# Up projections of two MLPs: five groups of 1024 columns each computed as seven half-size products, spread among plain tiles

## The chip, the cores and the metric

The kernel runs on one core of one Trainium2 chip. The metric is the time of one execution on the device in microseconds (us), median of several runs. TensorE (PE in the profile, with PEld for its weight loads) multiplies, VectorE (DVE) and ScalarE (ACT) work element by element, GpSimd (POOL) does little here, and SyncE (SP) issues the loads of the weights. SBUF is the memory that the engines read; PSUM holds the results of matmuls.

## The reference

The reference is a trunk of two layers on 256 tokens of width 2048, all in float32. Layer 0 mixes tokens by stick-breaking attention (mixer A), layer 1 by an attention over selected keys (mixer B). After each mixer comes an MLP with 8192 hidden features. The part that matters:

```python
for i in range(DEPTH):                      # 2 layers
    h = rms_norm(x, norm_mix[i])
    x = x + mixer(h, ...)                   # A in layer 0, B in layer 1
    h = rms_norm(x, norm_mlp[i])
    x = x + jnp.square(jax.nn.relu(h @ w_up[i])) @ w_down[i]
    # x (256, 2048), w_up (2048, 8192), w_down (8192, 2048)
```

## The kernel before

All weights pass through the core once, in pieces of 512 KB called items. An item is a tile of 128 partitions by 1024 float32 numbers. `load` (L674, its issue is L679) fetches it with SP's queue into one of five raw buffers (wraw). `split` (L681) takes it apart into a high part wh, which ScalarE writes by a copy that rounds (L82), and a low part wl, which VectorE writes as the difference (L689). Both lie in one buffer w, of which there are three. The matmuls then take x_hi·wh + x_hi·wl + x_lo·wh, which gives nearly float32 accuracy from three products in the rounded format. The activations are kept as high and low parts too.

There are two forms of item:

- `feats_out` (L201) gives features on partitions: the weights are stationary, 128 columns at a time, and x moves. An item covers four k-tiles and 256 columns: 8 pairs of a matmul of 512 columns (wh by x_hi and x_lo side by side, L211) and one of 256 (wl by x_hi, L212). It is used for the up projections and the features of the mixers.
- `tokens_out` (L178) gives tokens on partitions: x or h is stationary and the weights move. An item covers two k-tiles and 512 columns: 2 halves of the tokens x 2 k-tiles x 3 matmuls of 512 columns (L192 to L194).

In `mlp` (L250) the 8192 hidden features are taken in four parts of 2048. For each part come 32 up items (eight groups of 256 columns, four items each) and then 32 down items. When a group of the up projection is complete, `up_done` (L262) joins its two accumulators (ScalarE copy and VectorE add), squares the relu (VectorE), and writes high and low parts into hT (ScalarE, VectorE). hT is then stationary for the down projection. `down_done` (L272) adds the result to the residual stream xs, scaled by rs2, the square of the normalisation factor. The normalisation itself is left out of the MLP's operand and applied there, since relu squared is homogeneous. `prep` (L124) transposes xs with TensorE (L131) and writes xT, the split operand of the next projections.

The items of both layers stand in one list. The loop at the end of `trunk` walks through it: for item i it emits the split of item i + 2 (LEAD), the load of item i + 7 (LEAD + RAW), the matmuls of item i, and what has been put behind it (`post`). Only the first 16 items keep this order as written, and what is wrapped in `keep_in_program_order`; else a planner chooses the order of the instructions on each engine, by its own costs. PSUM has three accumulators of two banks (accp) and two of one bank (auxp).

The kernel's few lines that set the pace of an item:

```python
pair = wpool.tile([P, 2 * WT + BANK], F32R, name="w")        # three of these
copy(wh, raw)                                                # ScalarE
pin(dve.tensor_sub(wl, raw, wh.bitcast(F32)))                # VectorE
```

## Time and profile before

| what | value |
|---|---|
| runs, us | 2124.61, 2124.94, 2125.48; median 2124.94 |
| span of the profiled execution, first to last instruction | 2123.1 us |
| the profiled execution's own time | not listed apart; the runs lie 1.5 to 2.4 us above the span |
| TensorE busy | 2112.1 us, 99%, 10772 matmuls |
| VectorE busy | 1248.9 us, 59%, 1397 instructions |
| ScalarE busy | 1007.7 us, 47%, 1274 instructions |
| read from memory | 391.8 MB, 187 GB/s over the span |
| granted TensorE clock | 1.000 |

A row of a group names the line, the engine, the operation, what is written from what, the shapes and the count; then the busy time, the mean of one instruction in ns, and the idle time of the engine just before them with what ended it. A row of the timeline begins with start and duration in us. A row of windows gives a stretch, its length, and busy time with count of instructions for TensorE, its weight loads, VectorE, ScalarE and GpSimd, then the granted clock, the share of the DMA engines and GB/s. A row of waits says which engine and line waited for which, the total in us, how often, and the longest. A row of DMA issues ends with the KB of one and the median us from issue to landing. L82 is the line of the helper `copy`, which all ScalarE copies share.

### The profile page before, as it was taken

Reading aid. Unit: us, or ns where it says so; the run is one execution under the profiler, and the core shown is the slowest. Engines: PE = TensorE matmul, PEld = TensorE weight load, DVE = VectorE, ACT = ScalarE, POOL = GpSimd, SP = SyncE. Lnnn points to the kernel's source line nnn. Section 1 sums busy time; section 2 is a strip of 40 time slices with the busy share of each in tenths; the row PEclk is TensorE's granted clock in tenths of the full one; section 3 lists DMA queues with packets and bytes.
Section 4 is the critical chain, followed back from the end, with each engine's and each line's share of the span. In section 5 each row is a group of like instructions: output and inputs, shape, how many; then the busy total and the mean of one; then the engine's idle time right before and its main releaser. Section 6 shows DMA issues by size and latency. Waiting matters only on the chain.

```text
span 2123.1 us, 27404 instructions
## 1 busy us (share of the span) xinstructions
PE 2112.1 (99%) x10772; PEld 1800.8 (85%) x10772; DVE 1248.9 (59%) x1397; ACT 1007.7 (47%) x1274; POOL 28.3 (1%) x71
## 2 busy tenths in 40 slices
PE   8999999999999999999999999999999999999999
PEld 7888888888888888888888788888888888888887
DVE  5456665665565456456555877666555555555654
ACT  5455554544444444344454556555434434434443
POOL 0101100000000000000000000000000000000000
PEclk9999999999999999999999999999999999999999
DMA  7667655666666666666666565456666666666664
GB/s 238 189 194 192 180 165 177 184 190 194 193 189 192 194 190 190 194 190 189 193 213 183 159 193 164 149 179 188 193 194 189 191 193 191 190 195 192 188 205 151
DMA packets 298742, 398.93 MB, mean 188 GB/s; under 512 B 14578, under 2 KB 195444, under 8 KB 298612
## 3 DMA queue, kind: packets, MB, share of 16 engines
q1 hardware_dynamic: 290852, 389.74, 60.8%
q10 hardware_dynamic: 7760, 7.43, 1.3%
q8 instruction: 84, 1.38, 0.3%
q14 instruction: 46, 0.38, 0.1%
HBM read 391.82 MB, written 5.23 MB: 187 GB/s over the span
## 4 chain that ended last, share of the span: by engine, by line
PE 99%; DMA 0%; DVE 0%; ACT 0%; DVEq 0%; issue 0%
PE acc L211 29%; PE acc L192 17%; PE acc L193 17%; PE acc L194 17%; PE acc L212 15%; PE aux L131 1%; PE aux L589 0%; PE aux L193 0%; PE aux L194 0%; PE aux L192 0%; PE aux L370 0%; PE acc L326 0%; PE acc L503 0%; PE aux L606 0%; PE aux L567 0%; PE acc L468 0%
## 5 line engine op out<-in xcount | busy, mean ns | idle before, releaser
L689 DVE TENSOR_TENSOR w<-wraw,w 128x1024 fp32r<-128x1024 f32 x738 | 903.5, 1224 | 706.5 <-ACT w L82 697.0
L82 ACT ACTIVATE w<-wraw 128x1024 fp32r<-128x1024 f32 x738 | 782.4, 1060 | 835.5 <-PE acc L194 513.3
L211 PE MATMUL acc<-xT,w 128*128 128x512 f32 x2688 | 934.8, 390 | 0.0
L212 PE MATMUL acc<-xT,w 128*128 128x256 f32 x2688 | 759.0, 282 | 0.0
L211 PEld LDWEIGHTS acc<-xT,w 128*128 128x128 f32 x2688 | 504.6, 188 | 104.6
L212 PEld LDWEIGHTS acc<-xT,w 128*128 128x128 f32 x2688 | 508.0, 189 | 1.0
L192 PE MATMUL acc<-w,hT 128*128 128x512 f32 x992 | 386.3, 389 | 0.0
L194 PE MATMUL acc<-w,hT 128*128 128x512 f32 x992 | 386.2, 389 | 0.0
L193 PE MATMUL acc<-w,hT 128*128 128x512 f32 x992 | 385.9, 389 | 0.0
L194 PEld LDWEIGHTS acc<-w,hT 128*128 128x128 f32 x992 | 186.2, 188 | 38.7
L192 PEld LDWEIGHTS acc<-w,hT 128*128 128x128 f32 x992 | 186.2, 188 | 38.6
L193 PEld LDWEIGHTS acc<-w,hT 128*128 128x128 f32 x992 | 186.2, 188 | 38.2
L192 PE MATMUL acc<-w,xT 128*128 128x512 f32 x320 | 127.5, 399 | 2.5 <-ACT w L82 2.5
L193 PE MATMUL acc<-w,xT 128*128 128x512 f32 x320 | 126.5, 395 | 0.5 <-DVE w L689 0.5
L194 PE MATMUL acc<-w,xT 128*128 128x512 f32 x320 | 126.2, 394 | 0.0
L82 ACT ACTIVATE jc<-acc 128x512 f32<-128x512 f32 x84 | 50.4, 600 | 128.1 <-PE acc L212 128.0
L193 PE MATMUL acc<-w,oT 128*128 128x512 f32 x256 | 101.3, 396 | 0.0
L192 PE MATMUL acc<-w,oT 128*128 128x512 f32 x256 | 101.1, 396 | 0.0
L194 PE MATMUL acc<-w,oT 128*128 128x512 f32 x256 | 100.7, 394 | 0.0
L224 DVE TENSOR_TENSOR ju<-acc,jc 128x512 f32<-128x512 f32 x80 | 55.3, 691 | 77.0 <-ACT jc L82 77.0
L192 PEld LDWEIGHTS acc<-w,xT 128*128 128x128 f32 x320 | 60.6, 189 | 17.3 <-ACT w L82 2.9
L193 PEld LDWEIGHTS acc<-w,xT 128*128 128x128 f32 x320 | 60.5, 189 | 13.0 <-DVE w L689 1.0
(145 smaller groups left out, 1033.0 us busy)
## 6 DMA issues: line engine op xcount, KB each, us to landing
wraw<-in_w_up_dram SPq DMA_DIRECT2D x256, 512.0 KB, 3.8
wraw<-in_w_down_dram SPq DMA_DIRECT2D x256, 512.0 KB, 4.9
wraw<-in_w_in_a_dram SPq DMA_DIRECT2D x96, 512.0 KB, 4.3
wraw<-in_w_in_b_dram SPq DMA_DIRECT2D x64, 512.0 KB, 3.8
wraw<-in_w_out_a_dram SPq DMA_DIRECT2D x32, 512.0 KB, 3.7
wraw<-in_w_out_b_dram SPq DMA_DIRECT2D x32, 512.0 KB, 4.0
bv_d<-bv ACTq DMA_DIRECT2D x4, 766.0 KB, 9.0
bias<-bv_d ACTq DMA_DIRECT2D x4, 512.0 KB, 5.3
```

Of the source, the lines that this page charges most:

```text
L82: pin(act.activation(o, i, AF.Copy, scale=scale))
L131: pin(pe.transpose(ps[:, j, t * P:(t + 1) * P], xs[:, t, kt * P:(kt + 1) * P], ident))
L192: pin(pe.matmul(acc[t], L[:, k, 0, ts], wh[:, j, :], start=(k == 0), stop=False))
L193: pin(pe.matmul(acc[t], L[:, k, 0, ts], wl[:, j, :], start=False, stop=False))
L194: pin(pe.matmul(acc[t], L[:, k, 1, ts], wh[:, j, :], start=False, stop=(k == KT - 1)))
L211: pe.matmul(acc[:, m, :], wh[:, j, ms], xT[:, k, :, :], start=(k == 0), stop=False)
L212: pe.matmul(acc[:, m, 0:S], wl[:, j, ms], xT[:, k, 0, :], start=False, stop=(k == KT - 1))
L224: dve.tensor_add(u, acc[:, :, :S], c)
L689: pin(dve.tensor_sub(wl, raw, wh.bitcast(F32)))
```

## The change

Five groups of 1024 columns of each up projection are computed by Strassen's scheme in the variant with seven products and shared sums (Winograd's form). The operand x is cut in tokens (two halves of 128) and in k (two halves of 1024), the weights in k and in columns (two halves of 512). Instead of eight products of halves there are seven, of sums of quarters. The other 3072 columns of a layer remain plain: 1024 at the start, and 512 with each of the first four groups (hR).

- `forms` makes the four sums of x's quarters once per layer (xS, high and low parts), behind items 5 to 12 of the plain start.
- `seven` gives for a group 16 items (`first`) and 12 items (`second`), each with 6 matmuls of 512 columns with tokens on partitions. Per step of two k-tiles, four blocks of weights are loaded, b11 into wraw, b12, b22 and b21 into two new raw buffers (sraw). `sums` and `last_sum` replace blocks in place by sums on VectorE before they are split. A block can serve several items, so a raw buffer is given back only after its last use (`uses`, `loads`).
- Products that belong to several quarters of the result are kept apart in PSUM and combined on VectorE and ScalarE (`between`, `between2`, `after`, `after2`), squared (`square_up`), transposed by TensorE to features on partitions and split into hS (`turn`).
- The 28 half items of a group are spread among the down items of the group before and the plain up items (`spread`, SPANS). The down projection takes 1024 or 1536 rows at a time (hS, hR) in place of 2048.
- `prep` scales xs by the old normalisation factor before the MLP's transposes (two more ScalarE copies a chunk), and `stats` takes that out again.
- To make room in SBUF, some constants move to a pool that ends with the first section, RS moves into the sections, and smaller buffers are shared.

```diff
+HK = KT // 2
+LASTF = 5
+SPANS = {24: (11, 6), 32: (15, 8)}
+RAWS = {"wraw": RAW, "sraw": 2}
...
     def prep(c, col, squares=True, halves=(0, 1)):
 
+        block = [xs[:, t, c * 512:(c + 1) * 512] for t in range(2)]
+        if col >= 64:
+            for t in range(2):
+                even = tmp.tile([P, 2, S], F32, name="jc").rearrange("p a b -> p (a b)")
+                copy(even, block[t], scale=rs[:, t:t + 1])
+                block[t] = even
...
         def stats():
+            back = tmp.tile([P, 2], F32, name="back")
+            dve.reciprocal(back, rs)
             row_scale()
             sec["rs2"] = tmp.tile([P, 2], F32, name="rs2")
-            dve.tensor_mul(sec["rs2"], rs, rs)
+            dve.tensor_mul(sec["rs2"], rs, back)
+            dve.tensor_mul(sec["rs2"], sec["rs2"], sec["rs2"])
+        def whole(b, half):
+            t = sec["a", half] = temp().rearrange("p (k t) -> p k t", k=4)
+            ks = slice(HK * half + 4 * b, HK * half + 4 * b + 4)
+            dve.tensor_add(t, xT[:, ks, 0, :].bitcast(F32), xT[:, ks, 1, :].bitcast(F32))
+        def mixed(b, n):
...
+            if n == 0:
+                dve.tensor_sub(d(0), a21, a22)
+            elif n == 1:
+                dve.tensor_sub(d(1), d(0), a11)
+            elif n == 2:
+                dve.tensor_sub(d(2), a11, a21)
+            else:
+                dve.tensor_add(d(3), a12, d(1))
+        def parted(b, m):
+            d, x = sec["d", m], sec["xS"][:, 2 * m:2 * m + 2, 4 * b:4 * b + 4]
+            for n in range(2):
+                copy(x[:, n, :, 0, :], d[:, n])
+            for n in range(2):
+                dve.tensor_sub(x[:, n, :, 1, :], d[:, n], x[:, n, :, 0, :].bitcast(F32))
...
+        def seven(f, c0):
...
+            def item(raws, bank, x, s, source, opens=True):
+                def mm(wh, wl):
+                    acc = bank()
+                    on = dict(skip_group_check=not opens)
+                    for j in range(KB):
+                        k = KB * s + j
+                        pe.matmul(acc, x(k, 0), wh[:, j, :], start=opens and k == 0, stop=False, **on)
+                        pe.matmul(acc, x(k, 0), wl[:, j, :], start=False, stop=False, **on)
+                        pe.matmul(acc, x(k, 1), wh[:, j, :], start=False, stop=k == HK - 1, **on)
+                return Item(raws, KB, 512, mm, True, source)
...
+            for s in range(HK // KB):
+                b11, b12 = block(0, 0, s, "wraw"), block(0, 1, s, "sraw")
+                b21, b22 = block(1, 0, s, "sraw"), block(1, 1, s, "sraw")
+                def sums(s=s, b11=b11, b12=b12, b22=b22):
+                    t = g["t", s] = temp().rearrange("p (a b) -> p a b", a=KB)
+                    dve.tensor_add(b11.ap, b11.ap, b12.ap)
+                    dve.tensor_add(b12.ap, b12.ap, b22.ap)
+                    dve.tensor_add(t, b11.ap, b22.ap)
+                    return b12.ap
+                def last_sum(s=s, b21=b21):
+                    dve.tensor_add(b21.ap, g["t", s], b21.ap)
+                    return b21.ap
+                first += [item([b11], pair(0), quarter(0, 0), s, lambda b=b11: b.ap),
+                          item([b22, b12], single("v"), summed(3), s, lambda b=b22: b.ap),
+                          item([], pair(1), summed(2), s, sums),
+                          item([], single("z"), summed(0), s, lambda b=b11: b.ap)]
+                first[-2].uses = [b11, b12, b22]
+                first[-1].uses = [b11]
+                second += [item([b21], single("y"), quarter(1, 0), s, lambda b=b21: b.ap),
+                           item([], pair(0), summed(1), s, lambda s=s: g["t", s], False),
+                           item([], pair(1), quarter(1, 1), s, last_sum, False)]
+                second[-1].uses = [b21]
...
+            def between():
+                copy(se(0), pair(0)())
+                g["s5"] = flat("jc")
+                copy(g["s5"], g["z"])
+            def between2():
+                dve.tensor_sub(se(1), g["s5"], pair(1)())
+                dve.tensor_add(se(2), g["s5"], g["v"])
+            def after():
+                g["s2"] = flat("jc")
+                copy(g["s2"], pair(0)())
+                dve.tensor_sub(se(2), se(2), pair(0)())
+                dve.tensor_sub(se(1), se(1), pair(0)())
+            def after2():
+                dve.tensor_add(g["s2"], pair(1)(), g["s2"])
+                dve.tensor_add(se(0), g["y"], se(0))
+            def square_up(c):
+                dve.scalar_tensor_tensor(c, c, 0.0, c, op0=OP.max, op1=OP.mult)
+            def turn(c0, c1, kt):
+                h = h_tile(f, "hS")
+                ps = auxp.tile([P, 2, S], F32, name="aux")
+                for j in range(2):
+                    for t, c in enumerate((c0, c1)):
+                        cs = slice((kt + j) % 4 * P, ((kt + j) % 4 + 1) * P)
+                        pe.transpose(ps[:, j, t * P:(t + 1) * P], c[:, cs], ident)
+                hi = h[:, kt:kt + 2, 0, :]
+                copy(hi, ps)
+                dve.tensor_sub(h[:, kt:kt + 2, 1, :], ps, hi.bitcast(F32))
...
+        base = [0] + [1024 + 1536 * n for n in range(LASTF)]
+        items = up(0, "hS", 0, 4, 2)
         items[2 * QA + 1].post.append(stats)
+        todo = forms()
+        put(items, 5, [lambda n=n: (todo[2 * n](), todo[2 * n + 1]()) for n in range(8)])
+        for f in range(LASTF):
+            ds = down(f, base[f], ("hS",) if f == 0 else ("hS", "hR"))
+            if f + 1 < LASTF:
+                ds += up(f + 1, "hR", base[f + 1] + 1024, 2)
+            first, second, mid, ends = seven(f + 1, base[f + 1])
+            n1, n2 = SPANS[len(ds)]
+            items += spread(first, ds[:n1])
+            at = len(items) - 1
+            items += ds[n1:n1 + 2] + spread(second, ds[n1 + 2:n1 + 2 + n2])
+            put(items, at, mid)
+            at = len(items) - 1
+            items += ds[n1 + 2 + n2:]
...
+            for n, which in enumerate(((0, 1), (2,), (3, 4), (5,), (6, 7))):
+                items[at + n].post += [ends[e] for e in which]
+        items += down(LASTF, base[LASTF], ("hS",))
         return items, begin
...
+    def loads(done, most=None):
+        n, full = 0, set()
+        for raw in list(queue):
+            if n == most or raw.first > done + RAW + 3:
+                return
+            before = ahead[raw.tag]
+            if len(before) >= RAWS[raw.tag] and before[-RAWS[raw.tag]].last > done:
+                full.add(raw.tag)
+            if raw.tag not in full:
+                queue.remove(raw)
+                before.append(raw)
+                load(raw)
+                n += 1
```

More of the change, by code (lines that the diff above doesn't have):

```diff
@@ L99, in trunk @@
     dve.tensor_copy(tri, trif)
-    ones = consts.tile([P, P], F32R, name="ones")
+    ones = early.tile([P, P], F32R, name="ones")
     dve.tensor_copy(ones, onesf)
@@ L176, in rows, with tokens_out @@
         return w[r0:r0 + nr, c0:c0 + ncol].rearrange("(a p) c -> p a c", p=P)
-    def tokens_out(items, key, w, r0, c0, lhs, q, done, apart=False):
+    def tokens_out(items, key, w, r0, c0, lhs, q, done, n=KT, apart=False):
         def mm(wh, wl):
@@ new lines, in parted, with forms @@
+        def parted(b, m):
[4 more added lines that the diff above has]
+                dve.tensor_sub(x[:, n, :, 1, :], d[:, n], x[:, n, :, 0, :].bitcast(F32))
+        def forms():
+            out = []
+            for b in range(2):
+                out += [lambda b=b: whole(b, 0), lambda b=b: whole(b, 1)]
+                out += [lambda b=b, n=n: mixed(b, n) for n in range(4)]
+                out += [lambda b=b: parted(b, 0), lambda b=b: parted(b, 1)]
+            return out
@@ new lines, in up_done, with h_tile @@
+        def up_done(h, s, acc):
+            u = joined(acc)
+            dve.scalar_tensor_tensor(u, u, 0.0, u, op0=OP.max, op1=OP.mult)
+            hi = h()[:, 2 * s:2 * s + 2, 0, :]
+            copy(hi, u)
+            dve.tensor_sub(h()[:, 2 * s:2 * s + 2, 1, :], u, hi.bitcast(F32))
+        def h_tile(f, kind):
+            if (f, kind) not in sec:
+                n = {"hS": HK, "hR": 4}[kind]
+                sec[f, kind] = sec["pool"].tile([P, n, 2, S], F32R, name=kind, bufs=2 if kind == "hS" else 1)
+            return sec[f, kind]
@@ new lines, in down @@
+        def down(f, r0, kinds):
+            its, parts = [], [(k, i) for k in kinds for i in range({"hS": HK, "hR": 4}[k])]
+            n = len(parts)
+            for g in range(4):
+                for q in range(n // KB):
+                    tokens_out(its, ("dn", g), w_down[l], r0, 512 * g,
+                               lambda k, part, ts: sec[f, parts[k][0]][:, parts[k][1], part, ts], q,
+                               lambda acc, g=g: down_done(f, g, acc), n,
+                               apart=next_col is None and (f, g) == (LASTF, 3))
+            return its
@@ L272, in down_done @@
         def down_done(f, g, acc):
[L273 to L274 removed]
+            if f < LASTF or next_col is not None:
+                add_residual(g, next_col if f == LASTF else None, acc, sec["rs2"])
                 return
@@ L671, in trunk, with load, split @@
         n += len(its)
-    raws, parts = {}, {}
-    def load(i):
+    parts = {}
+    queue = []
+    for i, it in enumerate(items):
+        queue += it.raws
+        for raw in it.raws:
+            raw.first = i
+        for raw in getattr(it, "uses", it.raws):
+            raw.last = i
+    ahead = {tag: [] for tag in RAWS}
+    def load(raw):
+        home = wpool if raw.tag == "wraw" else now[0]
+        raw.ap = home.tile([P, WT], F32, name=raw.tag, bufs=RAWS[raw.tag])[:, :raw.a * raw.b].rearrange(
+            "p (a b) -> p a b", a=raw.a)
+        pin(nc.sync.dma_start(raw.ap, raw.src))
+    def loads(done, most=None):
[10 more added lines that the diff above has]
+                load(raw)
+                n += 1
+    def split(i):
         if i < len(items):
             it = items[i]
-            raws[i] = wpool.tile([P, WT], F32, name="wraw", bufs=RAW)[:, :it.a * it.b].rearrange(
-                "p (a b) -> p a b", a=it.a)
-            pin(nc.sync.dma_start(raws[i], it.src))
-    def split(i):
-        if i < len(items):
-            it, raw = items[i], raws.pop(i)
             pair = wpool.tile([P, 2 * WT + BANK], F32R, name="w")
@@ L697, in trunk @@
     for i in range(RAW):
-        load(i)
+        loads(-1, 1)
         if i == 0:
@@ L706, in trunk @@
         split(i)
-        load(RAW + i)
+        loads(i, 1)
     items[0].post.append(lambda: prep(0, 0, False, (1,)))
@@ L718, in trunk @@
         split(i + LEAD)
-        load(i + LEAD + RAW)
+        loads(i + LEAD)
         it.mm(*parts.pop(i))
```

155 lines of the change are left out of this document (104 added, 51 removed).

## Prediction

> **What bounds the kernel now.** I read the page's head and its chain of waits first, then what TensorE waited for, then its starts in both kinds of tile, and last VectorE.
>
> ```profile
> span 2123.1 us, 27404 instructions
> PE 2112.1 (99%) x10772; PEld 1800.8 (85%) x10772; DVE 1248.9 (59%) x1397; ACT 1007.7 (47%) x1274; POOL 28.3 (1%) x71
> PE 99%; DMA 0%; DVE 0%; ACT 0%; DVEq 0%; issue 0%
> PE acc L192 <- ACT w L82: 2.5, 1, 2.5
> PE acc L193 <- DVE w L689: 0.5, 1, 0.5
> ACT w L82 <- PE acc L212: 271.2, 174, 2.6
> ```
>
> The chain lies on TensorE, which after the first microseconds waited 3 us in all for a split weight tile (L192, L193). Splitting goes the other way: ScalarE waits for TensorE to give back one of three w buffers. So TensorE's own starts set the time. A busy TensorE is modelled with overlapping matmuls, so I take distances between starts, not durations. First and last rows of two stretches, down projection and up projection:
>
> ```profile
> 499.81 0.39 PE L194 MATMUL acc<-w,hT 128*128 128x512 f32 x1
> ...
> 511.82 0.39 PE L193 MATMUL acc<-w,hT 128*128 128x512 f32 x1
> ...
> 599.82 0.39 PE L211 MATMUL acc<-xT,w 128*128 128x512 f32 x1
> 600.05 0.28 PE L212 MATMUL acc<-xT,w 128*128 128x256 f32 x1
> ...
> 605.71 0.39 PE L211 MATMUL acc<-xT,w 128*128 128x512 f32 x1
> ```
>
> The first stretch holds 54 matmuls: 12.01/53 = 0.2266 us for 512 columns. The second holds 18 of L211: 5.89/17 = 0.3465 us for a pair of 512 and 256. A down item (12 matmuls) is 2.72 us, an up item (8 pairs) 2.77.
>
> The sum is made against the profiled execution: span 2123.1, and 1.5 to 2.4 us outside it, since the runs shown lie at 2124.61 to 2125.48 (the time of that very execution is not listed apart). I use the median, 2124.9, as span plus 1.8.
>
> **What the change takes from TensorE.** A group of 1024 columns is now 16 up items, 128 pairs: 44.35 us. After it is 28 half items of 6 matmuls of 512 columns (7 products, 8 k-tiles each, 3 matmuls a k-tile): 168 x 0.2266 = 38.07. Saved 6.28 a group, 62.8 over ten groups (five in each of two layers).
>
> **What it adds there.** The halves come out with tokens on partitions, so each group turns 16 tiles back in four blocks of four. The nearest rows are the turns of xs between matmuls:
>
> ```profile
> 1384.93 0.48 PE L192 MATMUL acc<-w,oT 128*128 128x512 f32 x1
> 1385.25 0.81 PE L131 MATMUL aux<-ident,xs 128*128 128x128 f32 x6
> 1385.82 0.48 PE L193 MATMUL acc<-w,oT 128*128 128x512 f32 x1
> 1386.14 0.39 PE L194 MATMUL acc<-w,oT 128*128 128x512 f32 x1
> ```
>
> From 1384.93 to 1386.14 is 1.21 us, of which two matmuls are 0.45, so six turns cost 0.76: 0.095 each and 0.19 for going in and out. Four cost 0.57, a group 2.28, all 22.8. Bounds: 15.2 without the going in and out; about 44 at the recorded 277 ns each, which pipelining excludes here. I take 22.8, the row that is the same operation. TensorE is left with 62.8 - 22.8 = **40.0 us less: 2085**, if it never waits.
>
> **What it adds on VectorE and ScalarE.** Rows for the pieces; the first four show VectorE's starts:
>
> ```profile
> 608.28 0.69 DVE L224 TENSOR_TENSOR ju<-acc,jc 128x512 f32<-128x512 f32 x1 [1.09 <-ACT jc L82]
> 609.01 0.69 DVE L267 SCALAR_TENSOR_TENSOR sq<-ju 128x512 f32<-128x512 f32 x1
> 609.62 1.22 DVE L689 TENSOR_TENSOR w<-wraw,w 128x1024 fp32r<-128x1024 f32 x1
> 610.75 0.68 DVE L270 TENSOR_TENSOR hT<-sq,hT 128x512 fp32r<-128x512 f32 x1
> ...
> L689 DVE TENSOR_TENSOR w<-wraw,w 128x1024 fp32r<-128x1024 f32 x738 | 903.5, 1224 | 706.5 <-ACT w L82 697.0
> L82 ACT ACTIVATE w<-wraw 128x1024 fp32r<-128x1024 f32 x738 | 782.4, 1060 | 835.5 <-PE acc L194 513.3
> L82 ACT ACTIVATE jc<-acc 128x512 f32<-128x512 f32 x84 | 50.4, 600 | 128.1 <-PE acc L212 128.0
> L559 DVE TENSOR_TENSOR nr<-nr,nry 128x1024 f32<-128x1024 f32 x5 | 6.1, 1221 | 0.1
> L233 DVE SCALAR_TENSOR_TENSOR xs<-acc,rs,xs 128x512 f32<-128x512 f32 x56 | 39.5, 747 | 11.3 <-PE acc L194 11.3
> ```
>
> An operation on 128x1024 takes 1.22 us as recorded but the next starts after 1.13; on 128x512 it is 0.69 recorded, 0.61 to the next start, 0.73 where the next needs the result. So every piece has two prices. A group's 28 splits and 16 sums of weight blocks (three in sums, one in last_sum, four times) are 44 x 1.13 = 49.7, and 14 operations at its end (between2, after, after2, the squares, the turns' low parts) x 0.65 = 9.1: 58.8 us (63.5 recorded), where 16 splits and four up_done were 16 x 1.13 + 12 x 0.65 = 25.9. The forms add 4 x 1.13 + 16 x 0.65 = 14.9 us a layer. VectorE so rises from 1249 by ten times 33 to 36 and 30, to some 1610 to 1640 of 2090 us: 78%, not the bound on average.
>
> Locally it is nearer. I call what lies between two groups' ends a period: 28 half items and the plain ones spread among them. Up_done costs 2.0 on VectorE, a finished down group 1.4:
>
> - first period (16 down, 8 up): TensorE 38.1 + 43.5 + 22.2 + 2.3 = 106.1; VectorE 58.8 + 24 x 1.13 + 4.0 + 5.6 = 95.5, 90% (103.0 recorded, 97%).
> - three periods of 24 down, 8 up: TensorE 127.9; VectorE 104.6, 82% (112.8, 88%).
> - last (24 down): TensorE 105.7; VectorE 91.5, 87% (98.9, 94%).
>
> ScalarE in the densest has 52 x 1.06, 7 x 0.60 and two up_done of 1.23: 62 of 106 us. No bound. Loads stay 16 of 512 KB a group; 40 in 106 us are 198 GB/s, beside 191 at a DMA share of 0.63 in this row, so bandwidth isn't the bound either:
>
> ```profile
> 1600.00:1800.00 200.00, 200.00 (x1038) 172.19 (x1037) 113.33 (x111) 88.78 (x93) 0.00 (x0) 1.00 0.63 191
> 1190.00:1200.00 10.00, 10.00 (x54) 7.77 (x51) 8.73 (x25) 5.89 (x8) 0.00 (x0) 1.00 0.44 117
> 1200.00:1210.00 10.00, 10.00 (x46) 8.27 (x45) 10.00 (x34) 4.14 (x5) 0.00 (x0) 1.00 0.67 201
> 1210.00:1220.00 10.00, 10.00 (x46) 8.29 (x45) 8.52 (x19) 4.65 (x6) 0.00 (x0) 1.00 0.71 204
> ```
>
> The last three rows are mixer B's top-k: VectorE 27.25 of 30 us busy (91%), once 10 of 10, and TensorE starts 46 matmuls in 10 us, no fewer than 0.2266 allows. Splits ran between the top-k operations:
>
> ```profile
> 1202.55 1.22 DVE L689 TENSOR_TENSOR w<-wraw,w 128x1024 fp32r<-128x1024 f32 x1
> ...
> 1204.08 0.62 DVE L525 MAX8 m<-sc 128x8 f32<-128x128 f32 x2
> ...
> 1205.25 1.22 DVE L689 TENSOR_TENSOR w<-wraw,w 128x1024 fp32r<-128x1024 f32 x1
> ```
>
> So 2.70 us apart, the pace of an item, while other work waited. The planner, which orders all this by itself, puts urgent splits ahead; I expect the same of sums and forms (forms bring 15 us of VectorE work into eight items, but nothing reads them before the second half item).
>
> **What a wait costs.** A split needs a w buffer back, then ScalarE, then VectorE:
>
> ```profile
> 602.15 1.06 ACT L82 ACTIVATE w<-wraw 128x1024 fp32r<-128x1024 f32 x1 [1.71 <-PE acc L212]
> 603.24 1.23 DVE L689 TENSOR_TENSOR w<-wraw,w 128x1024 fp32r<-128x1024 f32 x1 [1.54 <-ACT w L82]
> ```
>
> 602.15 to 604.47 is 2.32 us. With three buffers it may begin when the item three before ends and must be done when the one before ends: two items' time. Plain tiles give 5.44 - 2.32 = 3.1 us of slack; a half and a plain 4.08 - 2.32 = 1.8; two halves side by side 2.72 - 2.32 = 0.4. In-order VectorE has nothing behind a late operation but the next split, which TensorE waits for. By the order of spread, side-by-side halves occur 5 + 6 times in a dense period and 1 + 4 in the others: 37 a layer, 74 in all. Other work than splits holds VectorE for (95.5 - 52 x 1.13)/106 = 35% of a dense period; a running 1.13 us sum hurts when more than 0.4 of it is left (65%), by 0.37 on average: 74 x 0.35 x 0.65 x 0.37 = 6 us. Two more places, where a group's end is followed by the tiles that read it (turned hS, first item of down; after the last period only one plain item covers the turns), I put at 1 us a layer each: 4. Bounds: nothing, and 74 x 0.73 = 54 if each of those meets a whole sum. I take 10, near the top-k rows, where a fuller VectorE cost nothing.
>
> The even copies in prep are two more ScalarE copies of 128x512 per chunk of x at the mixers' ends. The last chunk is first read by the seventh item of the up projection, so six items, 16 us of matmuls, hide them; uncovered they would cost 1.4 us for the last chunk of each layer, 2.8 in all. The pool moves, RS's new place and the reciprocal in stats are off the path. The tail after the last matmul is unchanged.
>
> **Forecast**: 2124.9 - 40.0 + 10 = **2095**, its own range 2083 to 2108. Chance 0.62.
>
> **Rivals.**
> - *VectorE at its recorded durations.* If operations are held by each other so that the overlap of 0.09 us is lost, and 91% is the most that leaves TensorE fed, then the first period takes 103.0/0.91 = 113.2 (+7.1), the last 108.7 (+3.0), the plain start with forms (16 x 1.224 + 8.3 + 16.0 + 1)/0.91 = 49.3 against 44.3 (+5.0), the middle none: 15.1 a layer, 30 in all: **2115**. For: sums follow one another in place. Against: the top-k rows at 10 of 10. Chance 0.22, a third of it above 2120.7. The Trainium skill ("VectorE: DVE Perf Modes", The DRAIN you can't avoid) says a next operation does not start until the pipe has emptied, though one that isn't held starts earlier; by that rule alone this rival is the result. The trace agrees with the exception: 609.62 to 610.75 is less than 1.22.
> - *The two sraw buffers, a slower kernel.* b12 and b22 of the next step can be loaded only when the sums and the third item's split have read the old ones, and SP's queue holds later loads behind that wait. The loop: issue and landing, a second block behind it, split, two sums, copy, split. Landings:
>
> ```profile
> wraw<-in_w_up_dram SPq DMA_DIRECT2D x256, 512.0 KB, 3.8
> wraw<-in_w_down_dram SPq DMA_DIRECT2D x256, 512.0 KB, 4.9
> ```
>
> A block at full share is 0.524/(191/0.63) = 1.7 us, so 4.9 + 1.7 + 2.32 + 2.26 + 2.2 = 13.4 at most; with sums running before the second block's split less. TensorE's work per step is 4 x 1.36 + 2.75 x 2.72 = 12.9 in dense periods (16 steps), 15.6 in others (24). It decides from 15.4 on (16 x 2.5 = 40). At 16, with a load queued behind two others, it costs 16 x 3.1 + 24 x 0.4 = 59: **2144**. For: 13.4 exceeds 12.9 already. Against: such a chain must miss the prefetch in every step, and bandwidth is a third free. Chance 0.14.
> - *No waits at all, turns cheaper*: below 2083, chance 0.02.
>
> **How the numbers follow.** This kernel's runs tell 0.2% (4.2 us) from no change. Faster: 0.62 + 0.02 + two thirds of 0.22 = 0.79; within: 0.07; slower: 0.14. The range 2083 to 2127 leaves out 0.02 below and the slow rival above.
>
> **What would show it.** Pairs of L211 and L212 fall from 2688 to 1408 each, and 1680 matmuls of 512 columns stand in their place at 0.227 us: else the saving is wrong. Turns in four blocks of 0.57. VectorE at 76 to 79% of the span. TensorE's waits for w (from the split's sums) at 5 to 20 us in all, short, and mostly at side-by-side halves. I am wrong if those waits exceed 40 us, if SP's loads end them, if VectorE is full for whole periods, or if the turns cost twice as much.

## The result, and the profile after

The changed kernel takes 2104.05 us (median of 4 runs, 2102.72 to 2105.25). The kernel before, run beside it, takes 2125.06 (2124.61 to 2125.48). The ratio is 0.9901 with a 95% interval of 0.9887 to 0.9915: faster by 21 us, 1%. Forecast were 2095, a range of 2083 to 2108, and a gain of 30.

The head of the page with its chain, and three waits that the change could have touched, two of TensorE's and one of ScalarE's for a load (who waited for which, us in total, times, longest):

```profile
span 2101.4 us, 26497 instructions
PE 2080.6 (99%) x10052; PEld 1736.0 (83%) x10052; DVE 1614.7 (77%) x1773; ACT 1141.6 (54%) x1416; POOL 28.1 (1%) x71
PE 94%; DVE 4%; issue 1%; ACT 1%; DMA 0%; DVEq 0%; ACTq 0%
```

```profile
PE acc L217 <- DVE w L941: 9.3, 15, 1.9
PE acc L216 <- ACT w L100: 3.1, 3, 2.5
ACT w L100 <- DMA wraw<-in_w_up_dram: 1.7, 1, 1.7
```

L217 is the old L193, L941 the old L689 (VectorE's half of a split), L100 the old L82 (ScalarE's copies). The chain is still TensorE's, but 4% of it now runs over VectorE, where it was 0%. The wait for the low part of a weight tile has gone from 0.5 us to 9.3. For a load of the up projection ScalarE waited once, 1.7 us.

The groups of the pairs that remain, of the splits, and of the sums:

```profile
L941 DVE TENSOR_TENSOR w<-wraw,w 128x1024 fp32r<-128x1024 f32 x658 | 801.4, 1223 | 349.7 <-ACT w L100 342.9
L238 PE MATMUL acc<-xT,w 128*128 128x512 f32 x1408 | 494.7, 392 | 0.0
L239 PE MATMUL acc<-xT,w 128*128 128x256 f32 x1408 | 398.5, 284 | 0.0
...
L395 DVE TENSOR_TENSOR t<-wraw,sraw 128x1024 f32<-128x1024 f32 x40 | 48.7, 1218 | 0.0
L394 DVE TENSOR_TENSOR sraw<-sraw 128x1024 f32<-128x1024 f32 x40 | 48.8, 1220 | 0.3
```

L238 and L239 are the old L211 and L212: 1408 each, as predicted. Three windows (length; busy time and count of TensorE, weight loads, VectorE, ScalarE, GpSimd; clock, DMA share, GB/s): the stretch with `forms`, one inside the first period (from one group's first half item to the next group's), and one later on:

```profile
385.00:430.00 45.00, 45.00 (x247) 39.08 (x246) 39.00 (x56) 26.89 (x41) 0.00 (x0) 1.00 0.64 197
480.00:540.00 60.00, 57.99 (x268) 47.43 (x267) 51.68 (x52) 31.68 (x33) 0.00 (x0) 1.00 0.58 185
580.00:680.00 100.00, 100.00 (x478) 83.81 (x478) 83.17 (x83) 54.20 (x56) 0.00 (x0) 1.00 0.60 194
```

VectorE is 87, 86 and 83% busy. TensorE is idle in the middle one alone, for 2.01 us. So the idle time isn't spread over the dense stretches: it sits at single places. The worst of them, on VectorE, then ScalarE, then TensorE (start, duration):

```profile
480.22 1.23 DVE L393 TENSOR_TENSOR wraw<-wraw,sraw 128x1024 f32<-128x1024 f32 x1
481.37 1.22 DVE L941 TENSOR_TENSOR w<-sraw,w 128x1024 fp32r<-128x1024 f32 x1
482.50 1.22 DVE L394 TENSOR_TENSOR sraw<-sraw 128x1024 f32<-128x1024 f32 x1
483.64 1.22 DVE L395 TENSOR_TENSOR t<-wraw,sraw 128x1024 f32<-128x1024 f32 x1
484.77 1.41 DVE L260 SCALAR_TENSOR_TENSOR xs<-acc,rs,xs 128x512 f32<-128x512 f32 x2
486.09 1.22 DVE L941 TENSOR_TENSOR w<-wraw,w 128x1024 fp32r<-128x1024 f32 x1
...
481.94 1.07 ACT L100 ACTIVATE w<-wraw 128x1024 fp32r<-128x1024 f32 x1 [1.43 <-PE acc L218]
...
484.46 0.39 PE L216 MATMUL acc<-w,hS 128*128 128x512 f32 x1
484.95 0.50 PE L367 MATMUL acc<-w,xS 128*128 128x512 f32 x1
487.36 0.50 PE L217 MATMUL acc<-w,hS 128*128 128x512 f32 x1 [1.91 <-DVE w L941]
```

Two half items stand side by side here, then a plain one: the fourth step of the layer's first group. ScalarE has the plain tile's high part ready at 481.94 + 1.07 = 483.01. VectorE could start its difference at 483.64. It does the third sum (L395) and two residual adds of a plain group just ended (L260) first, and starts the difference at 486.09. From 484.95 TensorE could have started its next matmul 0.23 later; it starts at 487.36, 2.18 late. Yet t is read by the items of `second` only, many items later. The same place of layer 1 has the same gap. At the start of each group, where two halves stand side by side too, it is smaller; VectorE and TensorE at one of them:

```profile
681.70 1.22 DVE L395 TENSOR_TENSOR t<-wraw,sraw 128x1024 f32<-128x1024 f32 x1
682.84 0.68 DVE L251 TENSOR_TENSOR ju<-acc,jc 128x512 f32<-128x512 f32 x1
683.44 1.22 DVE L941 TENSOR_TENSOR w<-wraw,w 128x1024 fp32r<-128x1024 f32 x1
...
683.86 0.40 PE L367 MATMUL acc<-w,xS 128*128 128x512 f32 x1
684.71 0.50 PE L217 MATMUL acc<-w,hS 128*128 128x512 f32 x1 [0.45 <-DVE w L941]
```

A sum and the add of `up_done` (L251) stand ahead of the difference, and TensorE starts 684.71 - 683.86 - 0.23 = 0.62 us late. All ten groups begin with a gap of 0.40 to 0.63 us. In the second group of each layer it is ScalarE's high part that comes late, behind a copy of `up_done`; in the other eight it is the difference, as here.

Below, "gaps" are my own sums over the starts of all matmuls in the two MLPs: the time from one start to the next, above 0.2267 us for 512 columns and 0.1198 for 256. I list four parts: next to turns, single gaps over 0.2 us, those of 0.03 to 0.2, and the rest. Before they are 0.7, 0.0, 0.0 and 0.4 us; after 4.0, 14.9 (26 gaps), 6.1 and 2.7. They come to more than the profile's list of waits, which begins to count only when the recorded matmul has ended: the 2.18 and 0.62 us above stand there as 1.91 and 0.45.

By period, all gaps but those directly beside a turn are 0.3 us in the plain start of either layer, 4.3 and 5.9 (layer 0, layer 1) in the first period, 1.4 to 1.6 in each of the three middle ones, and 4.3 and 3.6 in the last. The first and the last are the densest, and have the most halves side by side.

### The profile page after: what moved, and what is told of

It is laid out like the page before. It is cut to its first block, busy times and chain, and to the rows that moved or that the text cites. A ratio compares the mean times of both kernels' runs of the same rounds, so it can differ in the third digit from the quotient of the medians.

```text
span 2101.4 us, 26497 instructions
## 1 busy us (share of the span) xinstructions
PE 2080.6 (99%) x10052; PEld 1736.0 (83%) x10052; DVE 1614.7 (77%) x1773; ACT 1141.6 (54%) x1416; POOL 28.1 (1%) x71
## 4 chain that ended last, share of the span: by engine, by line
PE 94%; DVE 4%; issue 1%; ACT 1%; DMA 0%; DVEq 0%; ACTq 0%
PE acc L217 17%; PE acc L218 17%; PE acc L216 17%; PE acc L238 15%; PE acc L239 8%; PE acc L368 3%; PE acc L369 3%; PE acc L367 3%; PE aux L368 2%; PE aux L369 2%; PE aux L367 2%; DVE w L941 2%; PE aux L449 1%; PE aux L156 1%; ACT w L100 1%
## 5 line engine op out<-in xcount | busy, mean ns | idle before, releaser
L941 DVE TENSOR_TENSOR w<-wraw,w 128x1024 fp32r<-128x1024 f32 x658 | 801.4, 1223 | 349.7 <-ACT w L100 342.9
L100 ACT ACTIVATE w<-wraw 128x1024 fp32r<-128x1024 f32 x658 | 698.2, 1061 | 577.9 <-PE acc L218 373.8
L238 PE MATMUL acc<-xT,w 128*128 128x512 f32 x1408 | 494.7, 392 | 0.0
L239 PE MATMUL acc<-xT,w 128*128 128x256 f32 x1408 | 398.5, 284 | 0.0
L238 PEld LDWEIGHTS acc<-xT,w 128*128 128x128 f32 x1408 | 264.0, 188 | 53.0
L217 PE MATMUL acc<-w,hS 128*128 128x512 f32 x752 | 295.7, 393 | 8.9 <-DVE w L941 8.9
L216 PE MATMUL acc<-w,hS 128*128 128x512 f32 x752 | 293.9, 391 | 0.6 <-ACT w L100 0.5
L218 PE MATMUL acc<-w,hS 128*128 128x512 f32 x752 | 293.8, 391 | 0.0
L239 PEld LDWEIGHTS acc<-xT,w 128*128 128x128 f32 x1408 | 266.0, 189 | 2.3 <-DVE w L941 0.6
L100 ACT ACTIVATE w<-sraw 128x1024 fp32r<-128x1024 f32 x160 | 170.0, 1063 | 156.8 <-PE acc L218 110.7
L941 DVE TENSOR_TENSOR w<-sraw,w 128x1024 fp32r<-128x1024 f32 x160 | 194.8, 1222 | 28.3 <-ACT w L100 26.5
L217 PEld LDWEIGHTS acc<-w,hS 128*128 128x128 f32 x752 | 141.6, 188 | 44.1 <-DVE w L941 15.3
L216 PEld LDWEIGHTS acc<-w,hS 128*128 128x128 f32 x752 | 141.6, 188 | 31.9 <-ACT w L100 2.3
L218 PEld LDWEIGHTS acc<-w,hS 128*128 128x128 f32 x752 | 141.6, 188 | 29.0
L217 PE MATMUL acc<-w,xT 128*128 128x512 f32 x320 | 126.2, 394 | 0.5 <-DVE w L941 0.5
L217 PE MATMUL acc<-w,oT 128*128 128x512 f32 x256 | 101.7, 397 | 0.0
L218 PE MATMUL acc<-w,hR 128*128 128x512 f32 x256 | 99.8, 390 | 0.0
L217 PE MATMUL acc<-w,hR 128*128 128x512 f32 x256 | 99.7, 389 | 0.0
```

The lines of the kernel that those rows point to most:

```text
L100: pin(act.activation(o, i, AF.Copy, scale=scale))
L216: pin(pe.matmul(acc[t], lhs(k, 0, ts), wh[:, j, :], start=(k == 0), stop=False))
L217: pin(pe.matmul(acc[t], lhs(k, 0, ts), wl[:, j, :], start=False, stop=False))
L218: pin(pe.matmul(acc[t], lhs(k, 1, ts), wh[:, j, :], start=False, stop=(k == n - 1)))
L238: pe.matmul(acc[:, m, :], wh[:, j, ms], xT[:, k, :, :], start=(k == 0), stop=False)
L239: pe.matmul(acc[:, m, 0:S], wl[:, j, ms], xT[:, k, 0, :], start=False, stop=(k == KT - 1))
```

## The experiments

The kernel before was timed beside each of these kernels, with medians from 2125.03 to 2125.36, so their times can be compared within a few tenths. "After" is 2104.05.

### The order of single operations: e1, e2, e3

The rows above name two culprits, the third sum and the closing work of plain groups. `e1_third_later` makes t at the split of a step's fourth item instead of its third, `e2_posts_later` emits the closing work of plain groups two items later, `e3_both_later` does both.

```diff
 # e1
-                    dve.tensor_add(t, b11.ap, b22.ap)
                     return b12.ap
+                def third(s=s, b11=b11, b22=b22):
+                    dve.tensor_add(g["t", s], b11.ap, b22.ap)
+                    return b11.ap
...
-                          item([], single("z"), summed(0), s, lambda b=b11: b.ap)]
+                          item([], single("z"), summed(0), s, third)]
...
 # e2
+            for it in ds:
+                it.late = bool(it.post)
...
+        for i, it in enumerate(items):
+            if getattr(it, "late", False):
+                items[i + 2].post.insert(0, it.post.pop(0))
```

> The third sum of each step (t = b11 + b22) is made at the split of the fourth half item instead of the third; nothing is left out. Theory 1 (order): TensorE's waits, 14 us in gaps of over 0.2, come from sums and group-end work that VectorE's queue holds ahead of the split that TensorE needs next; with the third sum out of that place most of the gaps of 0.6 at the ten group starts go, 4 to 9 us, so 2095 to 2100 us. Theory 2 (fullness): VectorE has too much to do beside half items whatever the order; the gaps only move, 2102 to 2106. Theory 3 (loads): b22 is held one item longer, so later loads make it slower, 2106 to 2112.

> The closing work of each plain group among the half items (residual adds, or the join and square of the up projection) is emitted two items later; nothing is left out. Theory 1 (order): the operation between the third sum and the late split goes away from there, 3 to 8 us less, 2096 to 2101, the two gaps of 2.2 us shrink by a residual pair of 1.3. Theory 2 (fullness): 2102 to 2106, since VectorE's total is the same. Theory 3 (loads): no change.

> Both of these moves together. Theory 1 (order): 2090 to 2097, gaps of over 0.2 us in the MLPs below 4 us in all. Theory 2 (fullness): 2101 to 2106. Theory 3 (loads): 2104 to 2112.

Measured: e1 2104.49 (0.9906, 0.9890 to 0.9923), e2 2098.78 (0.9878, 0.9863 to 0.9893), e3 2098.85 (0.9878, 0.9863 to 0.9893). VectorE at the same place in e1, where the third sum is L398:

```profile
484.55 1.22 DVE L398 TENSOR_TENSOR t<-wraw,sraw 128x1024 f32<-128x1024 f32 x1
485.69 1.40 DVE L260 SCALAR_TENSOR_TENSOR xs<-acc,rs,xs 128x512 f32<-128x512 f32 x2
487.01 1.21 DVE L944 TENSOR_TENSOR w<-wraw,w 128x1024 fp32r<-128x1024 f32 x1
```

The sum stands where it stood, ahead of the difference: the planner orders VectorE by itself, and emitting an operation an item later didn't move it. So e1 moved nothing and says nothing on what the sum's order is worth. The later closing work did move, and gained 5.3 us; the gaps over 0.2 us fell from 14.9 to 12.9 (e3: 9.8). The gaps of 0.6 at the starts of the middle groups, where L251 stood ahead of the difference, are gone; the two of 2.18, with L260, stayed. e2's profiled execution has one slow stretch of the clock more than that of after (1.6 us, see the last section). So e2 lies in the range of the order theory, but not because those two shrank, and e3 lies between the ranges of the two theories.

### What the sums and the turns cost: e4, e7

`e4_no_sums` leaves out the 160 sums: the splits take the blocks as they were loaded. `e7_no_turns` leaves out the 160 turns: ScalarE and VectorE write hS from the tiles as they lie, in two operations of half the size each.

```diff
 # e4
-                    t = g["t", s] = temp().rearrange("p (a b) -> p a b", a=KB)
-                    dve.tensor_add(b11.ap, b11.ap, b12.ap)
-                    dve.tensor_add(b12.ap, b12.ap, b22.ap)
-                    dve.tensor_add(t, b11.ap, b22.ap)
...
-                    dve.tensor_add(b21.ap, g["t", s], b21.ap)
...
 # e7
...
-                        pe.transpose(ps[:, j, t * P:(t + 1) * P], c[:, cs], ident)
-                hi = h[:, kt:kt + 2, 0, :]
-                copy(hi, ps)
-                dve.tensor_sub(h[:, kt:kt + 2, 1, :], ps, hi.bitcast(F32))
...
+                    part = c[:, kt % 4 * P:(kt % 4 + 2) * P].rearrange("p (j t) -> p j t", j=2)
+                    hi = h[:, kt:kt + 2, 0, ts]
+                    copy(hi, part)
+                    dve.tensor_sub(h[:, kt:kt + 2, 1, ts], part, hi.bitcast(F32))
```

> The 160 sums of weight blocks are left out: the splits take the blocks as loaded. VectorE has 181 us less. Theories 1 and 2 both: the waits of TensorE go, 14 to 18 us less, 2086 to 2090; what then remains above 2085 is not VectorE's sums. Theory 3 (loads): the gaps stay, 2100 to 2104.

> The 160 turns back on TensorE are left out: hS takes the untransposed tiles, with two copies and two differences of half the size in place of one each. The prediction priced the turns at 22.8 us: 2081. Without the 0.19 us of going in and out: 15.2, 2089. If a wait for the turned tiles costs more than the turns themselves, below 2080.

Measured: e4 2087.74 (0.9825, 0.9810 to 0.9840), e7 2087.85 (0.9824, 0.9811 to 0.9838). What is left of the wait in e4:

```profile
PE acc L217 <- DVE w L936: 1.2, 3, 0.5
```

The sums, which take no TensorE time at all, cost 16.3 us. With them gone the gaps are 3.8, 3.6 (12 gaps), 2.1 and 1.8, 16.4 less than after, and the kernel stands 2.7 us above the 2085 that the prediction gave for a TensorE that never waits. That 2085 counts the turns at 22.8 us; with the 16.2 measured here it is 2078, and e4 stands 9 above it, about what its gaps have more than those before. e4 takes 174 us of work from VectorE too (1440.7 us busy instead of 1614.7), so it can't tell a full VectorE from a badly ordered one. The turns cost 16.2 us, not 22.8.

### The same work elsewhere: e5, e8

`e5_spread_shift` changes only where the plain items stand among the halves: a group begins half, plain, half in place of half, half, plain, and the halves that stand side by side come at a later step (in the middle groups the third instead of the first). `e8_kept_order` is e3 with VectorE's splits, sums, residual adds and joins bound to the order in which the program emits them.

```diff
 # e5
-                while n < len(few) and (n + 1) * len(many) <= (i + 1) * len(few):
+                while n < len(few) and (n + 1) * len(many) <= (i + 1) * len(few) + len(many) // 2:
 # e8, beside e3's edits
+    def kept(ins):
+        if pinned[0] or i_now[0]:
+            tc.keep_in_program_order(ins)
...
-                    dve.tensor_add(b11.ap, b11.ap, b12.ap)
+                    kept(dve.tensor_add(b11.ap, b11.ap, b12.ap))
...
-            pin(dve.tensor_sub(wl, raw, wh.bitcast(F32)))
+            kept(dve.tensor_sub(wl, raw, wh.bitcast(F32)))
...
```

> The plain items stand half a step earlier among the half items, so that each group begins half, plain, half instead of half, half, plain; nothing is left out. Slack theory (a split behind two halves side by side has 0.4 us of slack, and the group start is where the first sums and the closing work meet such a pair): the gaps of 0.6 at group starts go, 4 to 8 us less, 2096 to 2100; some may come back where halves stand side by side elsewhere. Fullness theory (VectorE has too much to do wherever it is put): 2102 to 2106.

> As both moves together (third sum at the fourth half item's split, closing work two items later), and VectorE's splits, sums, residual adds and joins in the MLPs are bound to the order in which the kernel emits them, with the planner free in the rest; nothing is left out. Order theory: the two gaps of 2.2 us, which both moves left in place because the planner fills VectorE with what is ready, shrink below 1 us, and all gaps over 0.2 are below 6 us: 2091 to 2096. Fullness theory: the gaps move, 2097 to 2103. If a bound order makes VectorE wait for ScalarE where it had other work, slower than 2104.

Measured: e5 2125.44 (1.0002, 0.9993 to 1.0011), e8 2241.36 (1.0546, 1.0532 to 1.0560). In both VectorE does the same work as after (1614.3 us busy in e5). e5 loses the whole gain, which neither theory had, and e8 is 137 us slower than after. One of e5's gaps, on VectorE, ScalarE and TensorE:

```profile
590.15 1.22 DVE L394 TENSOR_TENSOR sraw<-sraw 128x1024 f32<-128x1024 f32 x1
591.29 1.22 DVE L395 TENSOR_TENSOR t<-wraw,sraw 128x1024 f32<-128x1024 f32 x1
592.42 1.22 DVE L941 TENSOR_TENSOR w<-wraw,w 128x1024 fp32r<-128x1024 f32 x1
...
589.60 1.06 ACT L100 ACTIVATE w<-wraw 128x1024 fp32r<-128x1024 f32 x1 [1.43 <-PE acc L218]
...
592.12 0.39 PE L216 MATMUL acc<-w,hS 128*128 128x512 f32 x1
592.60 0.51 PE L367 MATMUL acc<-w,xS 128*128 128x512 f32 x1
593.70 0.50 PE L217 MATMUL acc<-w,hS 128*128 128x512 f32 x1 [0.59 <-DVE w L941]
```

It is the picture of after, without closing work: the high part is there at 590.66, VectorE takes the third sum at 591.29 and the awaited difference at 592.42. TensorE loses 0.25 and 0.87 us here. Twelve places lose 1.1 to 1.4 us in this way and two 2.4; the gaps over 0.2 us are 56 with 31.6 in all. With the parts next to turns (7.3), 0.03 to 0.2 (7.4) and the rest (2.3) that is 48.6 against 27.7 after, which accounts for the 21 us. Not all of it is this picture: at group ends TensorE waits 6.4 us in six waits for turned tiles (hS), for which it has no wait on the list of after.

ScalarE's waits in e8 (L106 copies a block to its high part, L401 and L409 are sums):

```profile
ACT w L106 <- DVE sraw L401: 148.2, 40, 4.4
ACT w L106 <- DVE sraw L409: 111.2, 40, 3.8
```

Bound to the emitted order, a sum runs directly ahead of the split that reads it and behind everything emitted before. ScalarE waits for one 80 times, (148.2 + 111.2)/80 = 3.2 us on average, and the splits behind wait with it. Two further stops of TensorE's, 5.8 us each, lie in the plain starts, where `forms` and other work stand ahead of a split. The granted clock is lower here too, 0.988 over the span (see the last section). So neither order is good: the planner does sums too early for the splits beside them, the emitted order too late for their own readers.

### Another engine for a sum: e6

`e6_pool_third` gives the third sum to GpSimd, which is 1% busy.

```diff
-                    dve.tensor_add(t, b11.ap, b22.ap)
+                    pool.tensor_add(t, b11.ap, b22.ap)
```

> The third sum of each step is made on GpSimd instead of VectorE, 40 additions in all; nothing is left out. VectorE has 45 us less. Order and fullness theories both: a quarter of the sums' 16 us or more goes, since the third sum stands directly ahead of the late splits: 4 to 9 us less, 2095 to 2100. If GpSimd's additions slow VectorE's own or come too late for the second part, no gain or slower, 2103 to 2115.

Measured: 2159.69 (1.0162, 1.0148 to 1.0176), 56 us more than after and above every range given for it. Groups, and one such sum in the timeline:

```profile
L941 DVE TENSOR_TENSOR w<-sraw,w 128x1024 fp32r<-128x1024 f32 x160 | 238.7, 1496 | 31.2 <-ACT w L100 30.4
...
L394 DVE TENSOR_TENSOR sraw<-sraw 128x1024 f32<-128x1024 f32 x40 | 93.0, 2325 | 0.5
```

```profile
609.69 3.39 POOL L395 TENSOR_TENSOR t<-wraw,sraw 128x1024 f32<-128x1024 f32 x1 [15.30 <-DVE wraw L393]
...
609.59 1.23 DVE L394 TENSOR_TENSOR sraw<-sraw 128x1024 f32<-128x1024 f32 x1
610.73 3.43 DVE L941 TENSOR_TENSOR w<-sraw,w 128x1024 fp32r<-128x1024 f32 x1
614.08 1.21 DVE L941 TENSOR_TENSOR w<-wraw,w 128x1024 fp32r<-128x1024 f32 x1
```

The difference that VectorE starts at 610.73 ends at 614.16, 1.08 us after GpSimd's add has ended at 613.08: it got next to nothing done beside it. Over the 40 sums, L394 and the splits of sraw blocks are (2325 - 1220) x 40 + (1496 - 1222) x 160 = 88 us longer, where 40 x 1.22 = 49 were taken from VectorE. Splits are among the lengthened operations, and the largest of TensorE's waits is now a half item's for its low part, which after has once, for 0.2 us:

```profile
PE aux L368 <- DVE w L941: 26.7, 34, 1.3
```

### More slack instead of less work: e9, e10, e11, e12

If single operations ahead of a split are the trouble, a fourth w buffer, one item more of slack, should remove it with all the work in place. It needs room: `e9_three_w` is the control that makes the room and keeps three, `e10_four_w` uses it, `e11_four_w_lead3` emits splits three items ahead as well.

```diff
 # e9, e10, e11
-RAW = 5
+RAW = 4
...
-BANK = 128
+BANK = 8
...
-        u = tmp.tile([P, 2, S], F32, name="ju")
+        u = tmp.tile([P, 2, S], F32, name="ju", bufs=1)
...
 # e10, e11
-    wpool = ctx.enter_context(tc.tile_pool(name="wpool", bufs=3))
+    wpool = ctx.enter_context(tc.tile_pool(name="wpool", bufs=4))
 # e11
-LEAD = 2
+LEAD = 3
```

> The control for the next two: four raw buffers wraw instead of five, 8 instead of 128 spare columns behind each w buffer, one buffer ju instead of two; three w buffers as in the changed kernel, nothing left out. If none of these matters, 2102 to 2106. If the loads were near the path (theory 3), one raw buffer fewer makes it slower, 2108 or more.

> As the control, with four w buffers instead of three. Slack theory: a split may begin an item earlier, so the slack of a split behind two halves side by side rises from 0.4 to 1.8 us or more, a whole sum fits in it, and of the 24 us of gaps most go: 2086 to 2094. Order theory without slack (the planner puts what is ready ahead of splits, and it will do so with four buffers too): 2096 to 2106. A planned order that comes out badly, as in the shifted spread, is above 2110.

> As the one before (four w buffers), with the split of item i + 3 instead of i + 2 emitted ahead of item i's matmuls and closing work. Slack theory: 2085 to 2092. If the order of emission, which the planner takes for urgency, is what counts, this one is clearly below the one before, by 4 us or more. If neither counts, 2102 to 2106.

Measured: e9 2140.82 (1.0075, 1.0062 to 1.0087), e10 2128.15 (1.0014, 1.0005 to 1.0023), e11 2130.10 (1.0024, 1.0014 to 1.0034). Against its control the fourth buffer gains 12.7 us. Gaps above 0.03 us fall from 14.2 + 6.6 = 20.8 to 0.2, while those next to turns grow from 4.8 to 10.1. An earlier emission adds nothing.

The control is 37 us slower than after, though, with the same gaps. Its matmuls stand farther apart. Eleven starts in one item of the down projection, first in after, then in e9:

```profile
900.41 0.39 PE L217 MATMUL acc<-w,hS 128*128 128x512 f32 x1
...
902.68 0.39 PE L218 MATMUL acc<-w,hS 128*128 128x512 f32 x1
```

```profile
912.00 0.40 PE L217 MATMUL acc<-w,hS 128*128 128x512 f32 x1
...
914.33 0.40 PE L218 MATMUL acc<-w,hS 128*128 128x512 f32 x1
```

2.27 us over ten distances is 0.227, 2.33 is 0.233. Over the MLPs that makes the "rest" of e9 33.1 us instead of 2.7, and 32.9 of e10; the stretches outside the MLPs, which use the same buffers, take 10 us longer in e9. So e9 falls where the theory of loads had it and e10 where a badly planned order was expected, both for another reason, as e12 shows; e11 lies in none of its ranges. The suspect is BANK, the spare columns behind each w buffer, and with them the buffers' places. `e12_four_w_spaced` keeps BANK at 128, with four w buffers and four raw ones, and finds the room in single jc and ju buffers:

```diff
-RAW = 5
+RAW = 4
...
-    wpool = ctx.enter_context(tc.tile_pool(name="wpool", bufs=3))
+    wpool = ctx.enter_context(tc.tile_pool(name="wpool", bufs=4))
...
-        c = tmp.tile([P, 2, S], F32, name="jc")
-        u = tmp.tile([P, 2, S], F32, name="ju")
+        c = tmp.tile([P, 2, S], F32, name="jc", bufs=1)
+        u = tmp.tile([P, 2, S], F32, name="ju", bufs=1)
...
-                g["s2"] = flat("jc")
+                g["s2"] = temp()[:, :512]
...
```

> Four w buffers again, with the 128 spare columns behind each of them kept; the room comes from four wraw in place of five, one buffer each for jc and ju, and s2 in a buffer of the weight sums. Nothing is left out. Slack theory: the gaps over 0.03 us, 21 us of TensorE in the changed kernel, go as they did from the control to four buffers; some 5 us come back around the turns: 2085 to 2092. Matmuls of 512 columns stand 0.227 us apart as in the changed kernel if it was the spare columns that cost the control its time; if 0.231, it was the raw buffers or ju, and the time is 2115 to 2130.

Measured: 2088.66 us (0.9825, 0.9812 to 0.9838), 15 us less than after and the fastest kernel here that does all the work. Its page, the same window as above, and the waits of TensorE for a low part:

```profile
PE 2070.3 (99%) x10052; PEld 1738.5 (83%) x10052; DVE 1610.4 (77%) x1773; ACT 1137.2 (54%) x1416; POOL 28.0 (1%) x71
```

```profile
480.00:540.00 60.00, 60.00 (x286) 50.38 (x285) 53.85 (x56) 33.93 (x35) 0.00 (x0) 1.00 0.63 201
```

```profile
PE acc L218 <- DVE hS L452: 2.3, 2, 1.1
PE acc L217 <- DVE w L941: 1.1, 2, 0.6
```

VectorE is fuller in this window than after (53.85 us of 60, 90%) and TensorE stops nowhere in it. Gaps are 7.0 next to turns, 0.8, 0.8 and 1.2 us. The spacing is back at 0.227, with RAW at 4 and one ju buffer as in the control, so those two didn't cause the control's loss. BANK is what is left, by elimination; it was not changed alone, and the places of other buffers changed with it.

The first of the two waits above is for turned tiles: behind each layer's last group TensorE starts a matmul 1.31 us late. In layer 0 VectorE does two residual adds (1038.30 to 1039.71) ahead of the turn's low part, whose high part is there at 1038.44. e10 has the same two stops, after has none for hS. They are 2.6 us of what stands next to turns with four buffers.

The gaps of the main kernels side by side, in us (count of those over 0.2 in brackets):

| kernel | time | next to turns | over 0.2 | 0.03 to 0.2 | rest |
|---|---|---|---|---|---|
| before | 2125.06 | 0.7 | 0.0 (0) | 0.0 | 0.4 |
| after | 2104.05 | 4.0 | 14.9 (26) | 6.1 | 2.7 |
| e3, closing work later | 2098.85 | 3.8 | 9.8 (15) | 4.9 | 2.9 |
| e4, no sums | 2087.74 | 3.8 | 3.6 (12) | 2.1 | 1.8 |
| e5, other places | 2125.44 | 7.3 | 31.6 (56) | 7.4 | 2.3 |
| e8, bound order | 2241.36 | 16.5 | 102.8 (165) | 29.8 | 4.3 |
| e9, control | 2140.82 | 4.8 | 14.2 (28) | 6.6 | 33.1 |
| e10, control and four w | 2128.15 | 10.1 | 0.0 (0) | 0.2 | 32.9 |
| e12, four w | 2088.66 | 7.0 | 0.8 (1) | 0.8 | 1.2 |

The row of e8 leaves out its two stops of 5.8 us in the plain starts.

## Why the prediction was right or wrong

The direction, the saving and the overlap of the rest held; two terms of the sum were mis-sized, in opposite directions. That the total came within 9 us is in part luck: the turns were put some 5 to 7 us too high and the waits some 13 too low.

- **Saved on TensorE, 62.8: right.** The pairs fell to 1408 each. The account closes: 62.8, less the turns' own 160 x 0.089 = 14.3 (their spacing in the stream), less the gaps' growth of 26.6 (27.7 less 1.1), is 21.9; the span fell by 21.7. This is a sum over starts, not a separate experiment.
- **Turns, 22.8: too high.** By removal 16.2; in the starts 14.3 and 3.3 next to them, 17.6. The planner put them among matmuls in runs of one to eight, and a turn costs 0.089 in the stream and 0.02 beside it, where the row of the prediction gave 0.095 and 0.05.
- **Waits, 10: too low, and the step that failed.** The gaps away from turns grew by 23.3 (23.7 less 0.4). The profile's list, with 9.3 us for low parts, lies in the 5 to 20 that the prediction named as a sign, but it shows only part of the lost time. Removing the sums takes 16.3 us off; some 7 stay without them. The step was "The planner, which orders all this by itself, puts urgent splits ahead; I expect the same of sums and forms". It had been read from top-k rows, where splits were in time, but those were plain items with 3.1 us of slack, where an operation put ahead of a split need not show. The same order beside two halves, with 0.4 us of slack, did show. Of `forms` it was true (window 385 to 430: TensorE 45.00 of 45.00).
- **How the waits were estimated.** 74 places, hit at random, by 0.37 us on average. In fact the hits are systematic: a step's sums come up just where its two halves stand side by side, and closing work of plain groups falls due there too, so that the difference stands behind a sum and an add. All ten group starts show a gap of 0.40 to 0.63, and one further step of each layer one of 2.18. The side-by-side halves were named rightly as the weak places, the chance and the size of a hit weren't. The 4 us for tiles read at a group's end don't show in after as waits for hS; e12 has 2.6 us of them, after the last period.
- **The rival of a full VectorE, 2115: its number lay about as near (11 us off, the forecast 9), its reason falls.** It put 5.0 us into each plain start with `forms`, where TensorE lost 0.3 at 87%. It had the first and the last period as the costly ones (7.1 and 3.0), and they are (4.3 or 5.9, and 4.3 or 3.6), but the side-by-side halves are most frequent there too. What decides is e12: it runs 60 us at 90% without a stop, and about the same VectorE work gives 2088.66, 2104.05, 2125.44 or 2241.36 by buffers, places and order. The rule of the Trainium skill quoted with it ("VectorE: DVE Perf Modes", The DRAIN you can't avoid) shows here, too, in its exception: sums and splits in a row start 1.13 to 1.15 us apart at 1.22 recorded (480.22 to 484.77 above).
- **The rival of the sraw loop, 2144: falls.** No wait of TensorE's leads to a load of the up projection, ScalarE had one, of 1.7 us, and VectorE one, of 0.4. e12 has four wraw buffers instead of five, the same two of sraw, and is faster.
- **The theory of slack: borne out.** One more w buffer takes the gaps away from turns over 0.03 us from 20.8 to 0.2 in one pair of kernels (e9, e10) and from 21.0 to 1.6 in another (after, e12). In both the planner also laid some operations differently (in e12 the residual add at 484.50 stands behind the awaited difference), so the buffer's gain and the new order's can't be wholly parted.

Open remain three things: by what rule the planner orders VectorE (only its results were seen); why the time next to turns grows from 4.0 to between 7 and 10 with four buffers, beyond the 2.6 us of the two stops for turned tiles; and what in the w buffers' places sets the spacing of the matmuls.

## What to carry to other kernels

When tiles get shorter, count slack in microseconds before counting work: three buffers were three items of 2.7 us before, and here two of the items are 1.36 us long, so that a single operation of 1.13 us ahead of a split stops TensorE at an average load of 77%. Another buffer brought 15 us where moving single operations brought 5 and moving work to an idle engine lost 56. And an edit that needs room in the memory wants a control that makes the room only: without e9 the fourth buffer would have looked like a loss.

## What the hardware showed that I had not expected

- **GpSimd and VectorE shut each other out.** An add of GpSimd's on 128x1024 stretched VectorE's operation beside it from 1.22 to 3.43 us in the rows above; the 40 adds cost VectorE 88 us. In turn an add took GpSimd 2.40 us where it began just ahead of VectorE's operation (e6 at 689.48), and 3.39 where one of VectorE's was running. The Trainium skill ("SBUF — State Buffer", Who interferes with whom) says that an instruction of VectorE's with two SBUF inputs contends with a GpSimd instruction that reads SBUF, that the port pair they share is an exclusive lock, and that the order of issue decides who blocks. The trace agrees: VectorE's difference ends 1.08 us after GpSimd's add does.
- **Where the buffers lie seems to change a matmul's pace.** With 8 spare columns behind each w buffer instead of 128, matmuls of 512 columns start 0.233 us apart instead of 0.227, some 30 us over the MLPs, at equal work. Which part of the placement does it was not tried.
- **A stop of 2 us can be followed by a slower clock.** Behind the stop of 2.18 us in layer 1 six distances between matmuls are 0.42 to 0.43 us, and the granted clock over these 10 us is 0.83; behind the equal stop in layer 0 it is 1.00, with distances of 0.23. The two windows:

```profile
484.00:494.00 10.00, 8.00 (x34) 6.09 (x33) 8.03 (x8) 4.46 (x5) 0.00 (x0) 1.00 0.67 212
1490.00:1500.00 10.00, 7.99 (x28) 5.93 (x27) 6.73 (x7) 3.79 (x4) 0.00 (x0) 0.83 0.64 209
```

  The slow stretch costs some 1.6 us over the usual distances. Of 14 such stops in seven of these kernels, eight were followed by one. e8 stops most and has the lowest clock, 0.988; 0.012 of its 2240 us, some 27 us, is an estimate of what it lost by the clock. By what rule the clock falls, these runs don't show.
- **The placement of plain items alone is worth 21 us** (e5, its waits for turned tiles included), as much as the whole change brought.
